# A hybrid encoder on one core: attention scores in two matmuls over stacked query halves

## The chip, the cores and the metric

One core of a Trainium2 chip runs the whole program once. The metric is the device time of one execution in microseconds (us). TensorE multiplies matrices into PSUM (eight banks of 128 partitions by 512 words), VectorE and ScalarE read PSUM and SBUF, GpSimd (POOL) works on SBUF and also issues DMAs, and SyncE (SP) issues the loads of the weights.

## The reference, cut to what matters

Four layers, each a token mixer and a gated feed-forward with a short convolution, both behind an RMS norm and with a residual. Mixers: convolution, neighbourhood attention, retention, convolution. The change lies in the attention of the second layer (512 tokens on a grid of 8 rows by 64 columns, 16 heads of 64):

```python
q = rmsnorm(qkv[:, :, 0], q_g) * (NAT_HEAD_DIM ** -0.5)
k = rmsnorm(qkv[:, :, 1], k_g)
...
sc = jnp.einsum('bhqd,bhrqwd->bhqrw', q_r, k_win).astype(jnp.float32)
sc = sc + bias.transpose(0, 2, 1, 3)[None].astype(jnp.float32)
p = jax.nn.softmax(sc.reshape(b, NAT_HEADS, GRID_W, kh * NAT_KW), axis=-1)
...
return jnp.einsum('bhqrw,bhrqwd->bhqd', p, v_win)
```

A token sees all 8 rows and a window of 16 columns.

## The kernel before, in words

Every product of float32 values is made of float32r parts: a value is split into a high part (rounded by ScalarE) and a low part (the rest, by VectorE), and a product is high by high, high by low and low by high, three matmuls into one PSUM bank (`mm3`, lines 151 to 154; `mm3s`, lines 156 to 159, with the operands' roles exchanged; `split`, lines 161 to 163).

The activations stand transposed in SBUF, channels in the partitions. Weights come by SP's queue into two raw buffers (L138) and are split (L147, L148).

The attention stage (`nat`) takes the heads in four groups of four. The list `NORDER` gives the order in which the steps are written down: `p0 a0 p1 a1 p2 w0 a2 p3 a3 w1 w2 w3`, where `p` is a group's projection, `a` its attention and `w` its share of the output projection. Within that, a planner orders each engine's instructions: it runs through the program with a timing model and takes what is ready, in the order written down, so that matmuls of a later projection come between those of an attention. What each engine then runs is fixed before the start, and each engine takes its instructions in order.

- `proj` (L505): queries, keys and values of a group, 96 matmuls of 256 columns each (L157 to L159). Queries and keys are evacuated by ScalarE (L512) into `qk`, squared on POOL (L517), summed on VectorE (L518) and scaled on POOL (L531). The values are split, and two DMAs on POOL's queue make a copy `vs` shifted by 64 partitions (L544, L545).
- `att_prep` (L548): for each of the two head pairs of a group, TensorE transposes queries and keys (L555) into PSUM, two heads of 64 channels in 128 partitions. Keys become `kh` and `kl` (L558, L559). Queries become `qz`: for each head a tile with its own 64 rows filled and the other 64 rows zero, so that a product over all 128 rows takes one head alone. The zero rows are filled once, at the stage's start (L485 to L488), for two sets of tiles.
- `att_pair` and `att_step` (L569, L589): for each head and each half of the queries, two blocks of 128 queries by 256 keys: three matmuls each (L596), the bias with mask and the row's extreme in one VectorE instruction (L603), the exponential (L606), the scaling (L614), four transposes (L616), the split into `ph`, `pl`, and the product with the values.
- PSUM has three banks for projections and five for attention. All preparation of a group is written before its two pairs (`PRE`).
- `wout` (L637): a group's share of the output, with residual adds on VectorE (L234); the last one is followed by the norm for the feed-forward.

Of the kernel before, what the change touches and what calls it, by code (L numbers as in the profile page):

```python
# [8 lines left out]
F32 = mybir.dt.float32  # L9
F32R = mybir.dt.float32r  # L10
I32 = mybir.dt.int32
AF = mybir.ActivationFunctionType
ALU = mybir.AluOpType
AX = mybir.AxisListType
MUL, ADD, SUB = ALU.mult, ALU.add, ALU.subtract
PSUM = bass.MemoryType.PSUM

P = 128
T = 512
# [39 lines left out]
NORDER = "p0 a0 p1 a1 p2 w0 a2 p3 a3 w1 w2 w3".split()  # L59
NRAW = 2  # L60
HPO = 100000
NQZ = 2


@with_exitstack
def tile_trunk(
# [7 lines left out]
    nc = tc.nc  # L74
# [9 lines left out]
    def nm(s):  # L84
        uid[0] += 1
        return f"{s}{uid[0]}"
# [36 lines left out]
    def pc(name, i=0, w=1):  # L123
        c = COLS[name] + i
        if c < 64:
            return png[:, c:c + w]
        return pt[:, c:c + w]
# [23 lines left out]
    def mm3(o, wh, wl, ah, al, first, last):  # L151
        nc.tensor.matmul(o, wh, ah, start=first, stop=False)  # L152
        nc.tensor.matmul(o, wh, al, start=False, stop=False)  # L153
        nc.tensor.matmul(o, wl, ah, start=False, stop=last)  # L154
# [317 lines left out]
    def nat(after):  # L472
        PER = 4
        with ExitStack() as st:
            stage_pools(st, NTMP, *NPS)
            np1 = st.enter_context(tc.tile_pool(name=nm("nat"), bufs=1, reuse_waits=RW))
# [1 line left out]
            mask = np1.tile([P, 3, 256], F32, tag="mask", name=nm("mask"))  # L478
            nc.scalar.dma_start(mask, nmask.rearrange("p (v k) -> p v k", v=3))
            kstart = (0, 64, 192, 256)  # L480
            qzs = [[np1.tile([P, 2, T], F32R, tag=f"qz{n}{i}", name=nm("qz")) for i in range(2)]
                   for n in range(NQZ)]
            zz = np1.tile([P, 1], F32, tag="zz", name=nm("zz"))
            nc.vector.memset(zz, 0.0)
            for qz in qzs:  # L485
                for i in range(2):
                    zp = slice(64 - 64 * i, 128 - 64 * i)
                    nc.vector.tensor_copy(qz[i][zp], zz[zp].unsqueeze(2).broadcast_to([64, 2, T]))  # L488

            def part_proj(g, part):  # L490
                pss = [bank(psa), bank(psa)]
# [54 lines left out]
                return qk, va, vs  # L546

            def att_prep(g, pi, qk):  # L548
                qz = qzs[(2 * g + pi) % NQZ]
                kh = np2.tile([P, T], F32R, tag="kh", name=nm("kh"))  # L550
                kl = np2.tile([P, T], F32R, tag="kl", name=nm("kl"))
                for part in range(2):
                    ps = bank(psb)
                    for tb in range(4):
                        nc.tensor.transpose(ps[:, tb * P:(tb + 1) * P],  # L555
                                            qk[:, part, tb, pi * P:(pi + 1) * P], ident)
                    if part == 1:
                        nc.scalar.activation(kh, ps, AF.Copy, scale=pc("kg"))  # L558
                        nc.vector.scalar_tensor_tensor(kl, ps, pc("kg"), kh.bitcast(F32), MUL, SUB)  # L559
                    else:  # L560
                        for i in range(2):
                            r = slice(64 * i, 64 * i + 64)
                            nc.scalar.activation(qz[i][r, 0, :], ps[r], AF.Copy, scale=pc("qg")[r])
                            nc.vector.scalar_tensor_tensor(
                                qz[i][r, 1, :], ps[r], pc("qg")[r], qz[i][r, 0, :].bitcast(F32),
                                MUL, SUB)
                return qz, kh, kl

            def att_pair(g, pi, qz, kh, kl, va, vs):  # L569
                hi = np1.tile([P, T], F32R, tag="oh", name=nm("oh"), bufs=NO)  # L570
                lo = np1.tile([P, T], F32R, tag="ol", name=nm("ol"), bufs=NO)
                bms = []
                for i2 in range(2):
                    W = np2.tile([P, 384], F32, tag="W", name=nm("W"))
                    nc.sync.dma_start(W, wd[g * PER + pi * 2 + i2])
                    bm = np1.tile([P, 3, 256], F32, tag="bm", name=nm("bm"), bufs=NBM)
                    for vi, ws in enumerate((128, 64, 0)):
                        nc.gpsimd.tensor_tensor(bm[:, vi, :], W[:, ws:ws + 256],
                                                mask[:, vi, :], ADD)
                    bms.append(bm)  # L580
                for pr in range(2):
                    for i2 in range(2):
                        r = slice(64 * i2, 64 * i2 + 64)
                        c = slice(pr * 256, pr * 256 + 256)
                        op = att_step(pi, i2, pr, qz, kh, kl, bms[i2], va, vs)
                        split(op, hi[r, c], lo[r, c])
                return hi, lo

            def att_step(pi, i2, pr, qz, kh, kl, bm, va, vs):  # L589
                hh = pi * 2 + i2  # L590
                S = bank(psb)
                for i in range(2):
                    b = pr * 2 + i
                    ks = slice(kstart[b], kstart[b] + 256)
                    qs = slice(b * P, (b + 1) * P)
                    mm3(S[:, i * 256:(i + 1) * 256], qz[i2][:, 0, qs], qz[i2][:, 1, qs],  # L596
                        kh[:, ks], kl[:, ks], True, True)
                e = np1.tile([P, T], F32, tag="e", name=nm("e"), bufs=NE)
                mn, sx, rx = sm(2), sm(2), sm(2)
                for i in range(2):  # L600
# [490 lines left out]
```

## Time and profile before

| | us |
|---|---|
| median of three runs | 2616.24 (2616.24 to 2617.13) |
| profiled execution | 2615.78 |
| its span | 2614.0 |
| TensorE busy | 2583.8 |
| VectorE busy | 1643.6 |
| ScalarE busy | 1047.9 |
| POOL busy | 239.7 |

The span runs from the first to the last instruction of the profiled execution. Matmul times in the profile are pipelined and overlap: a matmul listed with 0.28 us can be followed by the next after less than half of that, and the distance between two starts tells what one costs. In a row of the timeline stand start, duration, engine, line, operation, the tiles out<-in, the shape, and in brackets the engine's idle time before it with what ended that. The attention stage runs from about 598 to 848 us of the span.

### The profile page before, as it was taken

The numbers are of one execution on the slowest core, as the hardware profiler recorded it, in microseconds if no ns is written. First come the engines' busy times: TensorE is split into PE (matmuls) and PEld (weight loads), VectorE is DVE, ScalarE is ACT, GpSimd is POOL, SyncE is SP. The second block draws the span as 40 slices with busy tenths as digits, with TensorE's granted clock in tenths as the row PEclk, the third lists the DMA queues.
The fourth block names the chain that finished last, engine by engine and source line by source line (L and its number), as shares of the span: only waits on it lengthen the run. The fifth ranks groups of instructions, "written<-read, shape, count | busy, mean of one in ns | idle before, by whom it ended". The sixth has DMA issues, their size and how long they took to land.

```text
span 2614.0 us, 32452 instructions
## 1 busy us (share of the span) xinstructions
PE 2583.8 (99%) x12830; PEld 2150.4 (82%) x12830; DVE 1643.6 (63%) x2628; ACT 1047.9 (40%) x1425; POOL 239.7 (9%) x253
## 2 busy tenths in 40 slices
PE   9989999999999999999999999999999998999999
PEld 7978888889998788888888888888888887888888
DVE  6766777437878777634656566677733667677732
ACT  5444444335655444423332423444432444444421
POOL 0104000003422000000000000100000100100000
PEclk9999999999999999999999999999999999999999
DMA  7624222333232222233222221322233652222232
GB/s 250 207 100 143 97 93 93 96 91 117 87 91 81 93 95 91 93 97 108 81 81 73 81 81 58 103 89 97 95 89 108 226 195 72 89 97 92 92 109 79
DMA packets 79784, 275.10 MB, mean 105 GB/s; under 512 B 10080, under 2 KB 13024, under 8 KB 79632
## 3 DMA queue, kind: packets, MB, share of 16 engines
q1 hardware_dynamic: 74304, 259.18, 30.4%
q0 software_dynamic: 4032, 11.14, 1.5%
q10 hardware_dynamic: 1296, 2.72, 0.3%
q8 instruction: 100, 1.64, 0.3%
q14 instruction: 52, 0.43, 0.0%
HBM read 263.04 MB, written 5.63 MB: 103 GB/s over the span
## 4 chain that ended last, share of the span: by engine, by line
PE 98%; DVE 1%; issue 0%; DMA 0%; ACT 0%; POOL 0%; SPq 0%; DVEq 0%; POOLq 0%
PE ps L154 27%; PE ps L152 27%; PE ps L153 27%; PE ps L393 3%; PE ps L158 3%; PE ps L159 3%; PE ps L157 3%; PE ps L396 1%; PE ps L289 1%; PE ps L290 1%; PE ps L294 1%; PE ps L616 0%; PE ps L437 0%; PE ps L842 0%; PE ps L555 0%
## 5 line engine op out<-in xcount | busy, mean ns | idle before, releaser
L147 ACT CAST wh<-wr 128x1024 fp32r<-128x1024 f32 (+1 forms) x410 | 423.2, 1034 | 1097.4 <-PE ps L153 801.0
L154 PE MATMUL ps<-xh,wl 128*128 128x512 f32 x1856 | 739.4, 398 | 0.0
L152 PE MATMUL ps<-xh,wh 128*128 128x512 f32 x1856 | 731.1, 394 | 6.3 <-ACT xh L201 6.3
L153 PE MATMUL ps<-xl,wh 128*128 128x512 f32 x1856 | 732.8, 395 | 0.0
L148 DVE TENSOR_TENSOR wl<-wr,wh 128x1024 fp32r<-128x1024 f32 (+1 forms) x406 | 493.3, 1215 | 329.1 <-ACT wh L147 326.8
L152 PEld LDWEIGHTS ps<-xh,wh 128*128 128x128 f32 x1856 | 349.1, 188 | 89.1 <-ACT xh L201 6.3
L153 PEld LDWEIGHTS ps<-xl,wh 128*128 128x128 f32 x1856 | 349.1, 188 | 87.7
L154 PEld LDWEIGHTS ps<-xh,wl 128*128 128x128 f32 x1856 | 349.0, 188 | 81.1
L152 PE MATMUL ps<-hh,wh 128*128 128x512 f32 (+1 forms) x726 | 281.6, 388 | 0.5 <-DVE x L316 0.5
L153 PE MATMUL ps<-hl,wh 128*128 128x512 f32 (+1 forms) x726 | 281.5, 388 | 0.0
L154 PE MATMUL ps<-hh,wl 128*128 128x512 f32 (+1 forms) x726 | 281.4, 388 | 0.0
L261 DVE TENSOR_TENSOR t<-ps,rstd_bc 128x512 f32<-128x512 f32 x176 | 120.9, 691 | 163.5 <-PE ps L154 163.5
L217 POOL TENSOR_TENSOR sqacc<-t,sqacc 128x512 f32<-128x512 f32 x49 | 77.5, 1581 | 1285.7 <-ACT t L215 1285.0
L152 PEld LDWEIGHTS ps<-hh,wh 128*128 128x128 f32 x726 | 136.8, 188 | 30.7 <-DVE x L316 0.7
L153 PEld LDWEIGHTS ps<-hl,wh 128*128 128x128 f32 x726 | 136.8, 188 | 30.1
L154 PEld LDWEIGHTS ps<-hh,wl 128*128 128x128 f32 x726 | 136.8, 188 | 30.0
L158 PE MATMUL ps<-wl,xh 128*128 128x256 f32 (+1 forms) x512 | 159.2, 312 | 0.6 <-DVE wl L148 0.6
L159 PE MATMUL ps<-wh,xl 128*128 128x256 f32 (+1 forms) x512 | 159.2, 312 | 0.0
L157 PE MATMUL ps<-wh,xh 128*128 128x256 f32 (+1 forms) x512 | 158.5, 312 | 0.0
L264 ACT ACTIVATE t<-t,par 128x512 f32<-128x512 f32 x176 | 142.5, 814 | 5.8 <-DVE t L261 5.7
L268 DVE SCALAR_TENSOR_TENSOR t<-t,par,t 128x511 f32<-128x511 f32 x176 | 132.1, 751 | 5.8
L393 PE MATMUL ps<-W,X 128*128 128x256 f32 x576 | 134.2, 331 | 0.6 <-DVE W L163 0.6
(227 smaller groups left out, 3470.1 us busy)
## 6 DMA issues: line engine op xcount, KB each, us to landing
wr<-in_f_up SPq DMA_DIRECT2D x176, 512.0 KB, 3.3
wraw<-in_cdw SPq DMA_DIRECT2D x64, 576.0 KB, 4.8
wr<-in_f_down SPq DMA_DIRECT2D x64, 448.0 KB, 3.3
wr<-in_f_down SPq DMA_DIRECT2D x32, 512.0 KB, 3.5
wr<-in_cw_in SPq DMA_DIRECT2D x30, 512.0 KB, 3.6
wr<-in_nat_qkv SPq DMA_DIRECT2D x24, 512.0 KB, 3.3
wr<-in_cw_out SPq DMA_DIRECT2D x16, 512.0 KB, 3.6
wr<-in_ret_qk SPq DMA_DIRECT2D x16, 512.0 KB, 3.2
```

What stands on the lines that cost most here:

```text
L147: nc.scalar.copy(hi[:, :n], raw[:, :n])
L148: eng.tensor_tensor(lo[:, :n], raw[:, :n], hi[:, :n].bitcast(F32), SUB)
L152: nc.tensor.matmul(o, wh, ah, start=first, stop=False)
L153: nc.tensor.matmul(o, wh, al, start=False, stop=False)
L154: nc.tensor.matmul(o, wl, ah, start=False, stop=last)
L157: nc.tensor.matmul(o, ah, wh, start=first, stop=False)
L158: nc.tensor.matmul(o, ah, wl, start=False, stop=False)
L159: nc.tensor.matmul(o, al, wh, start=False, stop=last)
L261: nc.vector.tensor_tensor(u, ps, rstd_bc, MUL)
L264: nc.scalar.activation(a, u, AF.Identity, bias=pc("fdb", l * 44 + c), scale=pt[:, w + 1:w + 2])
L268: nc.vector.scalar_tensor_tensor(a[:, :T - 1], u[:, 1:], pt[:, w + 2:w + 3], a[:, :T - 1], MUL, ADD)
L393: nc.tensor.matmul(o, X[:, b, 0, a:a + P], W[:, a].rearrange("p h n -> p (h n)"), start=a == 0, stop=False)
```

## The change

The scores of a head are made of two matmuls. The queries of a head stand in one tile `qs` of 128 rows: the high part in 64 rows and the low part in the other 64. The keys of a head stand twice, above one another: `ks` holds in both halves of the partitions the same 64 channels, high part and low part beside one another. Queries (high over low) times key high parts, plus queries times key low parts, gives the three products and the low by low product as well.

Keys are evacuated into a staging tile `kt` (one buffer), and four DMAs on POOL's queue copy it into the two `ks` tiles of the pair. VectorE writes the query low parts into the other half of the partitions. Keys are prepared before queries. The zero fills go away.

```diff
-            qzs = [[np1.tile([P, 2, T], F32R, tag=f"qz{n}{i}", name=nm("qz")) for i in range(2)]
-                   for n in range(NQZ)]
-            zz = np1.tile([P, 1], F32, tag="zz", name=nm("zz"))
-            nc.vector.memset(zz, 0.0)
-            for qz in qzs:
-                for i in range(2):
-                    zp = slice(64 - 64 * i, 128 - 64 * i)
-                    nc.vector.tensor_copy(qz[i][zp], zz[zp].unsqueeze(2).broadcast_to([64, 2, T]))
...
             def att_prep(g, pi, qk):
-                qz = qzs[(2 * g + pi) % NQZ]
-                kh = np2.tile([P, T], F32R, tag="kh", name=nm("kh"))
-                kl = np2.tile([P, T], F32R, tag="kl", name=nm("kl"))
-                for part in range(2):
+                qs = [np2.tile([P, T], F32R, tag=f"q{i}", name=nm("q")) for i in range(2)]
+                ks = [np2.tile([P, 2, T], F32R, tag=f"k{i}", name=nm("k")) for i in range(2)]
+                kt = np1.tile([P, 2, T], F32R, tag="kt", name=nm("kt"))
+                halves = (slice(0, 64), slice(64, 128))
+                for part in (1, 0):
...
                     if part == 1:
-                        nc.scalar.activation(kh, ps, AF.Copy, scale=pc("kg"))
-                        nc.vector.scalar_tensor_tensor(kl, ps, pc("kg"), kh.bitcast(F32), MUL, SUB)
+                        nc.scalar.activation(kt[:, 0], ps, AF.Copy, scale=pc("kg"))
+                        nc.vector.scalar_tensor_tensor(
+                            kt[:, 1], ps, pc("kg"), kt[:, 0].bitcast(F32), MUL, SUB)
+                        for i in range(2):
+                            for r in halves:
+                                nc.gpsimd.dma_start(ks[i][r], kt[halves[i]])
                     else:
-                        for i in range(2):
-                            r = slice(64 * i, 64 * i + 64)
-                            nc.scalar.activation(qz[i][r, 0, :], ps[r], AF.Copy, scale=pc("qg")[r])
+                        for i, r in enumerate(halves):
+                            nc.scalar.activation(qs[i][r], ps[r], AF.Copy, scale=pc("qg")[r])
                             nc.vector.scalar_tensor_tensor(
-                                qz[i][r, 1, :], ps[r], pc("qg")[r], qz[i][r, 0, :].bitcast(F32),
+                                qs[i][halves[1 - i]], ps[r], pc("qg")[r], qs[i][r].bitcast(F32),
                                 MUL, SUB)
...
-                    mm3(S[:, i * 256:(i + 1) * 256], qz[i2][:, 0, qs], qz[i2][:, 1, qs],
-                        kh[:, ks], kl[:, ks], True, True)
+                    o = S[:, i * 256:(i + 1) * 256]
+                    nc.tensor.matmul(o, q[:, qs], k[:, 0, ks], start=True, stop=False)
+                    nc.tensor.matmul(o, q[:, qs], k[:, 1, ks], start=False, stop=True)
```

## Rows read from the trace of the kernel before

**Rows 1.** The page: busy time of the engines (share of the span, instructions), and the chain that ended last by engine.

```profile
PE 2583.8 (99%) x12830; PEld 2150.4 (82%) x12830; DVE 1643.6 (63%) x2628; ACT 1047.9 (40%) x1425; POOL 239.7 (9%) x253
...
PE 98%; DVE 1%; issue 0%; DMA 0%; ACT 0%; POOL 0%; SPq 0%; DVEq 0%; POOLq 0%
```

**Rows 2.** The table by stretch of the attention stage. Columns: stretch, its length, busy time (and instructions) of PE, PEld, DVE, ACT and POOL, granted clock of TensorE, DMA share, GB/s.

```profile
608.00:680.00 72.00, 71.51 (x653) 71.51 (x654) 56.34 (x150) 39.72 (x89) 28.36 (x30) 1.00 0.31 96
680.00:735.00 55.00, 55.00 (x505) 54.40 (x505) 44.58 (x119) 33.82 (x79) 19.62 (x22) 1.00 0.31 94
735.00:797.00 62.00, 62.00 (x535) 60.06 (x534) 49.02 (x127) 35.33 (x79) 18.42 (x22) 1.00 0.30 90
797.00:831.00 34.00, 34.00 (x228) 29.34 (x227) 32.60 (x88) 18.92 (x47) 6.46 (x9) 1.00 0.33 98
831.00:850.00 19.00, 14.73 (x90) 11.17 (x88) 14.89 (x23) 12.28 (x24) 8.94 (x5) 1.00 0.14 50
```

**Rows 3.** What TensorE waited for from 597 to 850 us: who, for whom, us in total, times, longest.

```profile
PE ps L152 <- DVE pl L163: 1.2, 2, 1.1
PE ps L158 <- DVE wl L148: 0.6, 1, 0.6
PE ps L616 <- DVE e L614: 0.6, 1, 0.6
PE ps L152 <- ACT oh L162: 0.5, 1, 0.5
```

**Rows 4.** The timeline of TensorE in the first group: two score matmuls in succession.

```profile
638.22 0.28 PE L153 MATMUL ps<-kl,qz 128*128 128x256 f32 x1
638.34 0.28 PE L154 MATMUL ps<-kh,qz 128*128 128x256 f32 x1
```

**Rows 5.** The timeline of TensorE in a projection: the first and the last of 27 matmuls of the same shape that follow one another.

```profile
683.00 0.28 PE L158 MATMUL ps<-wl,xh 128*128 128x256 f32 x1
...
686.05 0.28 PE L159 MATMUL ps<-wh,xl 128*128 128x256 f32 x1
```

**Rows 6.** The table by stretch of the matmuls that read the padded queries `qz`: busy time and number on PE, granted clock, DMA share, GB/s.

```profile
608.00:680.00 72.00, 6.59 (x48) 1.00 0.31 96
680.00:735.00 55.00, 6.90 (x48) 1.00 0.31 94
735.00:797.00 62.00, 7.20 (x48) 1.00 0.30 90
797.00:831.00 34.00, 7.01 (x48) 1.00 0.33 98
```

**Rows 7.** The timeline of VectorE at the start of the attention stage.

```profile
598.20 5.10 DVE L488 CAST qz<-zz 64x1024 fp32r<-64x1024 f32 x4
...
607.21 1.23 DVE L148 TENSOR_TENSOR wl<-wr,wh 128x1024 fp32r<-128x1024 f32 x1
```

**Rows 8.** Timelines around the groups: on PE the last matmul of the first group's attention, the second group's transposes, the place from which its scores follow one another, the first of its later scores, the last matmul of the third group's attention and the fourth group's first transposes; on DVE and POOL the second group's preparation.

```profile
674.80 0.22 PE L154 MATMUL ps<-ph,va 128*64 128x128 f32 x1
...
680.78 1.91 PE L555 MATMUL ps<-ident,qk 128*128 128x128 f32 x16
...
683.99 0.74 DVE L564 SCALAR_TENSOR_TENSOR qz<-ps,par,qz 64x512 fp32r<-64x512 f32 x1
684.65 0.73 DVE L559 SCALAR_TENSOR_TENSOR kl<-ps,par,kh 128x512 fp32r<-128x512 f32 x1
...
686.28 0.55 POOL L544 DMA_DIRECT2D vs<-va  x1 [8.89 <-DVE va L163]
...
689.82 0.28 PE L152 MATMUL ps<-kh,qz 128*128 128x256 f32 x1
...
706.03 0.28 PE L152 MATMUL ps<-kh,qz 128*128 128x256 f32 x1
...
776.84 0.22 PE L154 MATMUL ps<-ph,va 128*64 128x128 f32 x1
...
785.62 0.60 PE L555 MATMUL ps<-ident,qk 128*128 128x128 f32 x4
```

**Rows 9.** The two copies of the values on POOL's queue, by line: number, duration of the issue in ns (min/median/max), and the time from issue to landing.

```profile
L544 POOL DMA_DIRECT2D vs<-va x4: 551/551/592, 635.4 to 799.9; - x4
...
DMA to landing us min/median/max: 3.6/3.7/6.6
...
L545 POOL DMA_DIRECT2D vs<-va x4: 534/538/542, 636.0 to 800.5; - x4
...
DMA to landing us min/median/max: 4.9/5.3/7.8
```

**Rows 10.** The timeline of VectorE in the last group, between the transposes and the first softmax step.

```profile
797.70 0.74 DVE L564 SCALAR_TENSOR_TENSOR qz<-ps,par,qz 64x512 fp32r<-64x512 f32 x1
...
803.59 0.41 DVE L603 CUSTOM_DVE_ANT_0 e<-ps,bm 128x256 f32<-128x256 f32 x1
```

**Rows 11.** Timelines of VectorE and POOL in the first group's softmax: two pairs of scalings, and what POOL ran beside the second.

```profile
641.01 0.61 DVE L614 TENSOR_SCALAR e<-e,sm 128x256 f32<-128x256 f32 x2
...
642.68 1.39 DVE L614 TENSOR_SCALAR e<-e,sm 128x256 f32<-128x256 f32 x2
642.84 1.09 POOL L517 TENSOR_TENSOR t<-qk 128x512 f32<-128x512 f32 x1 [6.33 <-ACT qk L512]
```

**Rows 12.** All waits for a DMA on POOL's copies in the convolution stages: us in total, times, longest.

```profile
ACT X L162 <- DMA xf<-u: 11.2, 10, 2.8
```

More of the change, by code (lines that the diff above doesn't have):

```diff
@@ L61 @@
 HPO = 100000
-NQZ = 2
 @with_exitstack
@@ L557, in att_prep, with att_pair @@
                     if part == 1:
-                        nc.scalar.activation(kh, ps, AF.Copy, scale=pc("kg"))
-                        nc.vector.scalar_tensor_tensor(kl, ps, pc("kg"), kh.bitcast(F32), MUL, SUB)
-                    else:
-                        for i in range(2):
-                            r = slice(64 * i, 64 * i + 64)
-                            nc.scalar.activation(qz[i][r, 0, :], ps[r], AF.Copy, scale=pc("qg")[r])
+                        nc.scalar.activation(kt[:, 0], ps, AF.Copy, scale=pc("kg"))
[4 more added lines that the diff above has]
+                                nc.gpsimd.dma_start(ks[i][r], kt[halves[i]])
+                    else:
+                        for i, r in enumerate(halves):
+                            nc.scalar.activation(qs[i][r], ps[r], AF.Copy, scale=pc("qg")[r])
                             nc.vector.scalar_tensor_tensor(
-                                qz[i][r, 1, :], ps[r], pc("qg")[r], qz[i][r, 0, :].bitcast(F32),
+                                qs[i][halves[1 - i]], ps[r], pc("qg")[r], qs[i][r].bitcast(F32),
                                 MUL, SUB)
-                return qz, kh, kl
-            def att_pair(g, pi, qz, kh, kl, va, vs):
+                return qs, ks
+            def att_pair(g, pi, qs, ks, va, vs):
                 hi = np1.tile([P, T], F32R, tag="oh", name=nm("oh"), bufs=NO)
@@ L584, in att_pair, with att_step @@
                         c = slice(pr * 256, pr * 256 + 256)
-                        op = att_step(pi, i2, pr, qz, kh, kl, bms[i2], va, vs)
+                        op = att_step(pi, i2, pr, qs[i2], ks[i2], bms[i2], va, vs)
                         split(op, hi[r, c], lo[r, c])
                 return hi, lo
-            def att_step(pi, i2, pr, qz, kh, kl, bm, va, vs):
+            def att_step(pi, i2, pr, q, k, bm, va, vs):
                 hh = pi * 2 + i2
```

## The prediction

> **What bounds the kernel now.** I read the page's totals first, then the chain, then a table by stretch of the attention stage, then TensorE's waits in it. TensorE is busy 2583.8 of 2614.0 us and is 98% of the chain that ended last [rows 1]: an instruction taken from it pays wherever no other wait stands behind it, and one added elsewhere costs nothing until TensorE waits for it. The average is not enough, because the change lies in one stage of some 250 us. The table by stretch [rows 2] parts that stage. From 608 to 797 us TensorE is busy almost without a break, with VectorE at 78 to 81%: this part is TensorE's. From 797 to 831 both are full: VectorE is busy 32.60 of 34.00 us, so there a shorter TensorE stream leaves VectorE's work as it is. From 831 to 850 TensorE is idle for 4 us behind the last softmax. TensorE's listed waits from 597 to 850 sum to 2.9 us [rows 3], none of them for a DMA.
>
> **The change part by part.**
>
> *Removed: one matmul of three in every score.* 16 heads by 4 query blocks by 3 make 192 score matmuls; 128 stay. The 0.28 us beside each is a pipelined time; what one costs is the distance between starts. Two score matmuls start 0.12 us apart [rows 4]; the same shape in the projection has 26 distances between 683.00 and 686.05 us [rows 5], so 3.05 / 26 = 0.1173 us each. The new matmuls have this shape too (128 rows by 128 columns, 256 moving), so 64 x 0.1173 = 7.5 us leave TensorE. Each of four stretches holds 48 of the 192 [rows 6]: three are TensorE's (48 removed, 5.6 us); the last is the full one (16 removed, 1.9 us), of which I count nothing.
>
> *Removed: four fills of the zero padding.* They hold VectorE from 598.20 to 603.3; the root of the mean square and the low half at 607.21 stand behind them [rows 7]. TensorE works on meanwhile and waits only 0.6 us for that low half [rows 3]. So 5.1 us of VectorE are worth 0.6 us.
>
> *Moved: keys before queries.* In the second group's evacuations VectorE makes a query low half at 683.99 and the first key low half at 684.65 [rows 8]. With keys first, the key takes the 683.99 place and ends at 684.7, 0.7 us earlier, which pays for part of what follows. The number of these instructions stays: two for keys, four for queries in each pair.
>
> *Added: 32 copies on the POOL queue*, four for each of eight pairs, 64 partitions by 4096 bytes, 256 KB each. The nearest rows are the two 384 KB copies of the values on this queue: 0.55 and 0.54 us to issue; the first lands 3.7 us after its issue (3.6 to 6.6), the second 5.3 (4.9 to 7.8) [rows 9]. The second is issued 0.55 later, so it adds 5.3 + 0.55 - 3.7 = 2.15 us for 384 KB, or 1.4 us for 256 KB. From that I estimate the first key copy down after 3.7 - 0.7 = 3.0 us, the second 4.4, the third 5.9, the fourth 7.3. Head 0 of a pair needs the first two, head 1 all four. In the second group: 684.7 + 4.4 = 689.1 for head 0, where before the bulk of the scores began at 689.82 [rows 8]. In the last group the first low half after the transposes sits at 797.70 on VectorE and ends at 798.4; + 4.4 = 802.8, and before the first softmax step on VectorE was at 803.59 [rows 10]. In between VectorE has other low halves, a value split and residual adds to do, and the row at 803.59 names no idle time before it, so it does not run dry. Both ends for all 32: nothing, if other matmuls cover the wait; and, if every group's first score stood still for 7.8 - 3.7 = 4.1 us (from the median landing of the first row to the longest of the second), 16.4 us in four groups. I take nothing, the value nearest to rows 3, where no DMA holds TensorE.
>
> *Added: a wait on ScalarE.* The staging tile has one buffer, so the second pair of a group writes its key only when the first pair's four copies are down, 7.3 us later. Behind that instruction stand weight halves and exponentials on ScalarE, and one bank of the five stays taken. But the second pair's scores come late anyway: in the second group the last three of eight steps started only at 706.03 [rows 8]. The ends are nothing (the order is planned with the wait in view) and 7.3 us in each of four groups, 29 in all. I take nothing, because a group's attention ends well before the next group's transposes: 674.80 to 680.78 us and 776.84 to 785.62 [rows 8], 6 and 9 us to spare.
>
> *POOL itself* was busy 239.7 us of the span [rows 1]; 32 x 0.55 = 17.6 us of issuing come to it. Before the second group's value copies it had been idle for 8.89 us, waiting for a low half of the values [rows 8]; key copies put behind those in POOL's queue would wait too. Its ends are nothing and 17.6 us; I take nothing for the idle time.
>
> *A rule weighed.* Beside a POOL product of 1.09 us two of VectorE's scalings of the exponentials take 1.39 us instead of 0.61 [rows 11]: the two engines shut each other out. The Trainium skill (SBUF — State Buffer, "SBUF: two separate sides") goes further: while VectorE runs an operation in a two-port mode, GpSimd cannot write the descriptors of a DMA issued from its queue; the same page, under "A bandwidth-pool intuition that's wrong", has 620 ns alone against some 3100 ns. By that, the first copies of four groups would come 10 us late in all, an estimate from that page, and the sum below would end at 2620. In this trace VectorE runs evacuations and splits, not scalings, where a group's first copies fall [rows 10].
>
> **Sum.** -5.6 (three groups) - 0.6 (fills) + 0 = -6.2 us. The profiled execution took 2615.78 us, 1.78 more than its span of 2614.0, so 2609.6; the median of the runs, 2616.24, stands 0.46 above it: **2610.0 us**.
>
> **The rivals.**
> 1. *The copies are partly late.* For it: in the convolution stage ScalarE waited ten times for a like copy from POOL, 11.2 us in all, 1.1 each, 2.8 the longest [rows 12], so the planned order reckons such copies somewhat early; and the value copies may stand ahead in POOL's queue. Against it: none of those waits is among TensorE's in rows 3. At 1.1 us in each of four groups the gain is 6.2 - 4.4 = 1.8: 2614.4 us, which can't be told from no change.
> 2. *Slower: the copy of the keys becomes the bound.* The place is a group's first score on TensorE, which takes its instructions in order, so all behind it stands still. The price is the 4.1 us above in each of four groups: 2616.24 - 6.2 + 16.4 = 2626.4. Above 1.55 us a group it eats the gain; from 2.85 us a group it is slower by 0.2%. For it: landings of 6.6 and 7.8 us are in rows 9, and ScalarE's wait for the staging tile can hold weight halves back. Against it: the 6 and 9 us to spare in rows 8.
> 3. *Slower in another way: POOL and VectorE shut each other out* while the second head's and the second pair's copies are issued. Each of four issues would stand behind one pair of scalings, 4 x 1.39 = 5.6 us [rows 11]; in the two groups with the fewest other matmuls that is 11.1 us: 2616.24 - 6.2 + 11.1 = 2621.1. It is what that rule of the Trainium skill (SBUF — State Buffer) comes to here. Against it: the value copies in rows 9 were mostly down in 3.7 and 5.3 us.
> 4. *The last stretch gains too*, if VectorE's backlog there gets shorter because the work in front of it starts earlier: 2610.0 - 1.9 = 2608.1.
>
> That the change does not do what it says is hardly possible: a matmul that is not issued takes no time. The order of all engines is planned anew, though, and for that I allow 3 us either way.
>
> **How the numbers follow.** A difference of 0.2%, 5.2 us, is about what a measurement of this kernel can tell from none: faster is below 2611.0, slower above 2621.5. Chances: the forecast 0.36, with a range of its own from 2607 to 2613; rival 1 0.36; rival 2 0.15; rival 3 0.03; rival 4 0.10. Faster is rival 4 and all but a small edge (0.02) of the forecast, 0.44; same is rival 1 and that edge, 0.38; slower is rivals 2 and 3, 0.18. The range goes below to rival 4 less the 3 us for a changed order, 2605, and above into rival 2 as far as 3.0 us in each of four groups, 2622.
>
> **What would show it.** The score lines should hold 128 matmuls 0.117 us apart, the fills be gone, and TensorE's waits between 597 and 850 name no key copy. The time from the last group's transposes to the stage's end should be as before; the 6 us should lie ahead of them. TensorE waiting for a key tile or its DMA by over 1 us a group speaks for rival 1 or 2; ScalarE waiting on the staging tile with weight halves late behind it would show my zero for that wait wrong; VectorE idle ahead of the last group's first softmax would show the backlog argument wrong.

## The result, and the profile after

The changed kernel takes 2622.28 us (median of 20 runs, 2617.73 to 2625.64) against 2616.37 for the kernel before: ratio 1.0021, 95% interval 1.0014 to 1.0027, 5.9 us slower. The forecast was 2610.0 with a range up to 2622, and slower had a chance of 0.18: the sign was wrong, and the time lies just outside the range. The spread of the 20 runs goes with TensorE's mean granted clock in each, from 2617.7 us at 0.997 to a median of 2624.8 in the four runs at 0.994.

The page of the changed kernel, busy times and the chain by engine, against [rows 1]:

```profile
PE 2583.5 (99%) x12766; PEld 2145.1 (82%) x12766; DVE 1641.5 (63%) x2623; ACT 1045.3 (40%) x1425; POOL 257.2 (10%) x285
...
PE 93%; DVE 4%; DMA 1%; ACT 1%; issue 1%; POOL 0%; SPq 0%; ACTq 0%; POOLq 0%; DVEq 0%
```

64 matmuls are gone (12830 to 12766), and TensorE's busy time is what it was. The idle rest of the span grew from 30.2 to 37.3 us, and the busy time is a union of pipelined matmuls, which hides that some stand further apart. The chain tells it: TensorE's share fell from 98% to 93%, and VectorE, DMA and ScalarE came in.

The table by stretch, columns as in [rows 2]:

```profile
608.00:680.00 72.00, 69.75 (x619) 67.51 (x618) 54.44 (x148) 37.80 (x87) 32.55 (x37) 1.00 0.44 125
680.00:735.00 55.00, 53.88 (x493) 52.82 (x492) 43.66 (x117) 32.13 (x77) 27.41 (x32) 1.00 0.46 125
735.00:797.00 62.00, 58.50 (x484) 55.50 (x483) 49.34 (x125) 31.62 (x74) 22.17 (x30) 0.97 0.48 128
797.00:831.00 34.00, 32.74 (x193) 27.62 (x193) 29.68 (x63) 17.86 (x39) 9.63 (x17) 1.00 0.66 163
```

The stretches are the same times, not the same work. In each of these TensorE now has gaps (3.5 us in the third, none before), and the DMA engines carry more than before: 0.44 to 0.66 against 0.30 to 0.33. What the gaps wait for, TensorE's waits from 590 to 870 us, against [rows 3]:

```profile
PE ps L592 <- DMA k<-kt: 4.9, 4, 3.2
PE ps L612 <- DVE e L610: 3.3, 8, 1.1
PE ps L288 <- DVE x L233: 2.2, 1, 2.2
PE ps L151 <- DVE pl L162: 1.8, 5, 0.7
```

The first line is new: scores (L592) wait for the DMA that copies the keys. The second had 0.6 us, once; now the transposes of the scaled exponentials wait eight times. (The third, behind the last residual add, stands with the same 2.2 us in all kernels below, third_off among them, and is no part of the change.) The copies by their line, with the time from issue to landing:

```profile
L555 POOL DMA_DIRECT2D k<-kt x32: 509/529/604, 633.1 to 816.4; - x32
...
  ACT kt L550: 11.4, 3
  PE ps L592: 4.9, 4
...
DMA to landing us min/median/max: 2.9/5.1/10.0
```

The 4.9 us are not the whole. Read from both timelines, the time from the start of a group's main block of transposes to its first score matmul, in the four groups (in the first and the fourth, the kernel before had run four of the sixteen transposes 9 us ahead of that block):

```
before   5.9   5.4   4.5   5.3 us
after   10.1  10.2  12.1  10.4 us
```

By that measure each group's scores start 4 to 8 us later. TensorE has other work for most of that, but the softmax that follows on VectorE starts later too. The first projection matmul and the last output matmul of the stage, in the kernel before and in the changed one:

```profile
594.44 0.28 PE L157 MATMUL ps<-wh,xh 128*128 128x256 f32 x1
847.60 0.39 PE L154 MATMUL ps<-oh,wl 128*128 128x512 f32 x1
...
594.34 0.28 PE L156 MATMUL ps<-wh,xh 128*128 128x256 f32 x1
854.57 0.40 PE L153 MATMUL ps<-oh,wl 128*128 128x512 f32 x1
```

The stage grew from 253.2 to 260.2 us, although the 7.5 us of removed matmuls are gone: some 14.6 us of distance between TensorE's starts came in.

The third group is the worst. POOL's timeline there, and TensorE's:

```profile
738.48 0.55 POOL L535 DMA_DIRECT2D vs<-va  x1 [5.42 <-DVE va L162]
739.03 0.54 POOL L536 DMA_DIRECT2D vs<-va  x1
739.74 2.02 POOL L555 DMA_DIRECT2D k<-kt  x4 [0.17 <-issue]
```

```profile
745.46 0.40 PE L153 MATMUL ps<-oh,wl 128*128 128x512 f32 x1
749.05 0.42 PE L592 MATMUL ps<-k,q 128*128 128x256 f32 x1 [3.20 <-DMA k<-kt]
749.28 0.42 PE L593 MATMUL ps<-k,q 128*128 128x256 f32 x1
...
749.92 0.63 PE L151 MATMUL ps<-oh,wh 128*128 128x512 f32 x1
750.35 0.63 PE L152 MATMUL ps<-ol,wh 128*128 128x512 f32 x1
```

Two value copies left just ahead of the key copies; the keys of the first head landed at 748.96, 9.2 us after 739.74. In the other groups it was 5.3, 5.1 and 6.1 us, where the prediction had 4.4. The table over the wait and what follows it, columns as before:

```profile
740.00:745.60 5.60, 5.60 (x28) 4.45 (x26) 5.22 (x8) 3.10 (x4) 1.76 (x4) 1.00 1.09 243
745.60:749.00 3.40, 0.25 (x2) 0.00 (x0) 1.84 (x3) 0.00 (x0) 0.00 (x0) 1.00 1.08 237
749.00:752.50 3.50, 3.45 (x11) 2.90 (x12) 0.78 (x4) 0.21 (x1) 0.00 (x0) 0.53 0.32 89
752.50:756.00 3.50, 3.50 (x30) 3.50 (x29) 3.08 (x7) 2.52 (x6) 0.13 (x1) 0.98 0.18 28
```

While the copies were under way, with a weight load on SP's queue beside them, the DMA engines were full (1.09 and 1.08). And after its 3.2 us of idleness TensorE ran at a granted clock of 0.53, the 1.2 GHz level, for 3.5 us: the products with 512 columns start 0.43 us apart instead of 0.235. From 749.05 to 752.48 it did four scores and six of these, which at the full clock take 4 x 0.117 + 6 x 0.235 = 1.88 us: 1.55 us more for the one wait.

### The profile page after: what moved, and what is told of

Read it like the earlier page. It is cut to its first block, busy times and chain, and to the rows that moved or that the text cites. A ratio compares the mean times of both kernels' runs of the same rounds, so it can differ in the third digit from the quotient of the medians.

```text
span 2620.8 us, 32404 instructions
## 1 busy us (share of the span) xinstructions
PE 2583.5 (99%) x12766; PEld 2145.1 (82%) x12766; DVE 1641.5 (63%) x2623; ACT 1045.3 (40%) x1425; POOL 257.2 (10%) x285
## 3 DMA queue, kind: packets, MB, share of 16 engines
q1 hardware_dynamic: 74304, 259.18, 30.2%
## 4 chain that ended last, share of the span: by engine, by line
PE 93%; DVE 4%; DMA 1%; ACT 1%; issue 1%; POOL 0%; SPq 0%; ACTq 0%; POOLq 0%; DVEq 0%
PE ps L153 26%; PE ps L151 26%; PE ps L152 26%; PE ps L392 4%; PE ps L158 2%; PE ps L156 2%; PE ps L157 2%; PE ps L395 1%; DMA k<-kt 1%; DVE e L610 1%; DVE wl L147 1%; PE ps L288 1%; PE ps L289 1%; PE ps L293 1%; PE ps L436 0%
```

## The experiments

The theory behind the experiments was that the time from a ready key to its landing is what is paid. Rivals: issuing on POOL, the wait for the staging tile, the order keys before queries, and the stacked layout itself.

**no_copies**: the changed kernel without copies; both heads read the evacuated keys.

```diff
-                ks = [np2.tile([P, 2, T], F32R, tag=f"k{i}", name=nm("k")) for i in range(2)]
-                kt = np1.tile([P, 2, T], F32R, tag="kt", name=nm("kt"))
+                kt = np2.tile([P, 2, T], F32R, tag="kt", name=nm("kt"))
+                ks = [kt, kt]
...
-                        for i in range(2):
-                            for r in halves:
-                                nc.gpsimd.dma_start(ks[i][r], kt[halves[i]])
```

> The changed kernel without its 32 key copies and without the single staging buffer: both heads read the evacuated keys where they lie (two buffers). It leaves out that each head's keys stand in both halves, so its scores mix two heads; the 128 score matmuls, the stacked queries and the order keys before queries stay. Theory A (the copies: their landing, the staging buffer and the order planned around them cost some 14 us of the stage, more than the 7.5 us that the matmuls give): 2608 to 2611 us, and TensorE's idle time in the stage back near the kernel before. Theory B (the copies are not the cause: softmax on VectorE and the order of work bound the stage, so that fewer matmuls only turn into waits for the exponentials): 2616 us or more.

2614.24 us; ratio 0.9991 (0.9983 to 1.0). The copies cost 8.0 us. But the gain that remains, 2.5 us, is far from the forecast: something else is paid too. The first scores stand 7.0, 7.0, 5.9 and 5.9 us behind the transposes here, so 1 to 2 us of their delay in the changed kernel come without any copy.

**third_off**: the kernel before with two of its three matmuls; the product of the queries' low part is left out.

```diff
-                    mm3(S[:, i * 256:(i + 1) * 256], qz[i2][:, 0, qs], qz[i2][:, 1, qs],
-                        kh[:, ks], kl[:, ks], True, True)
+                    o = S[:, i * 256:(i + 1) * 256]
+                    nc.tensor.matmul(o, qz[i2][:, 0, qs], kh[:, ks], start=True, stop=False)
+                    nc.tensor.matmul(o, qz[i2][:, 0, qs], kl[:, ks], start=False, stop=True)
```

> The kernel before with zero padding and everything else as it was, but only two of the three matmuls of each score: the low part of the queries is left out (and still computed). It measures the removal by itself. Theory A: 64 x 0.117 = 7.5 us less, or 5.6 if the last group's part is not gained: 2609 to 2611 us. Theory B: within 2 us of 2616.

2608.71 us; 0.997 (0.9959 to 0.9982): 8.0 us less. By the profile the stage takes 245.9 us instead of 253.2, 7.3 less: all 64 matmuls count, those of the last stretch too.

**copies_3mm**: the kernel before, its padding and 192 matmuls kept, with keys first, a staging tile and four copies of 128 KB a pair.

```diff
-                for part in range(2):
+                for part in (1, 0):
...
+                            for r in halves:
+                                nc.gpsimd.dma_start(ks[r, i], kt[r, i])
```

> The kernel before with all its zero padding and 192 score matmuls, but keys evacuated first, into a staging tile of one buffer, and copied by four DMAs of a pair on the POOL queue into the tile that the scores read (64 partitions by 2048 bytes each, half the bytes of the changed kernel's). It measures the copies without the removal. Theory A: 2616 plus most of 14 us, 2625 to 2631; at half the bytes the landings are shorter, so 2622 is the lower end. Theory B: within 2 us of 2616.

2619.67 us; 1.001 (1.0001 to 1.0019): +2.9. Here no score waits for a DMA; its copies are half as large, those of the high parts leave before the low parts are made, and they land in 2.2 to 5.8 us, median 3.6. So not every copy costs 8 us, which comes back in the last pair of runs. The time fits neither theory, and the first scores come 8.2 to 9.3 us behind the transposes, nearly as late as in the changed kernel: a late first score alone doesn't set the price.

**inplace**: no staging tile; each head's keys are evacuated into their own half, one copy of 256 KB a head fills the other.

```diff
+                        for i, r in enumerate(halves):
+                            nc.scalar.activation(ks[i][r, 0], ps[r], AF.Copy, scale=pc("kg")[r])
+                            nc.vector.scalar_tensor_tensor(
+                                ks[i][r, 1], ps[r], pc("kg")[r], ks[i][r, 0].bitcast(F32), MUL, SUB)
+                            nc.gpsimd.dma_start(ks[i][halves[1 - i]], ks[i][r])
```

> The changed kernel without the staging tile: each head's keys are evacuated into their own half of the head's tile (one more ScalarE and one more VectorE instruction a pair, 0.69 and 0.74 us, 5.5 and 5.9 us in all), and one copy a head brings them to the other half: 16 copies instead of 32, half the bytes, and no wait of ScalarE for a staging buffer. Theory A, if the staging wait and the number of copies matter: 2611 to 2617 us, with ScalarE's wait for the copies gone. If the landing of the first copy alone matters: 2618 to 2622, since a group's first scores still stand behind a copy. Theory B: 2622 to 2626, for VectorE has more to do.

2622.7 us; 1.0022 (1.0012 to 1.0031), the same as the changed kernel with half the copies, and without ScalarE's 11.4 us of waiting for the staging tile. So no gain from ending that wait shows; since a pair has one more instruction here on ScalarE and one on VectorE, a small gain may be hidden. TensorE's wait for keys is still there, and larger:

```profile
PE ps L590 <- DMA k<-k: 7.8, 5, 2.9
```

**third_kfirst**: third_off with keys first (`for part in (1, 0)`).

> The kernel before without each score's third matmul (the queries' low part is left out of the scores, as in the run third_off, 2608.7 us) and with one line more: keys are evacuated before queries. Theory O (the order keys before queries costs some 5 us by itself, since all transposes of a group then wait for the keys, which are projected after the queries): 2613 to 2615 us, and the fourth group's sixteen transposes in one block after its value projection. Rival L (the order is free; what run no_copies lost against third_off comes from the stacked layout or its buffers): 2608 to 2610 us.

2613.14 us; 0.9987 (0.9978 to 0.9996). Against third_off the order costs 4.4 us, with no copy in the kernel; TensorE's waits for the split of the exponentials are 2.2 us instead of 0.5. **no_copies_qf** asks the same of the stacked layout: no_copies with queries first.

> Run no_copies (2614.2 us) with queries before keys; what it leaves out is the same, the key copies. If the order of keys and queries is worth the 4.4 us that third_kfirst and third_off lie apart, also in the stacked layout: 2608.5 to 2611 us. If the stacked layout or the missing fills hold something of their own: 2612 to 2615.

2608.28 us; 0.9969 (0.9958 to 0.998): 6.0 us under no_copies, and next to third_off. The stacked layout itself costs nothing.

**q_first**: the changed kernel with queries first.

> The changed kernel with one line different: queries are evacuated before keys, as in the kernel before. Theory O: 5 us less than the changed kernel, 2616 to 2619 us, less what the later start of the key copies gives back. Rival L, with the landing of the copies as the only price: the keys start 0.7 to 1.5 us later on ScalarE and VectorE in each of four groups, so 2622 to 2627 us.

2620.64 us; 1.0015 (1.0006 to 1.0024). Only 1.6 us come back, between the ranges of the two theories: the keys, and with them the copies, start later.

**early_keys**: key preparation and copies written ahead of the group's value projection.

```diff
+                kks = [key_prep(pi, qk) for pi in range(2)]
                 pvs = part_proj(g, 2)
```

> The changed kernel with the key half of the preparation (transposes, evacuation, copies) written ahead of the group's value projection instead of behind it, so that 11 us of projection matmuls stand between the copies and the scores; queries are prepared where they were. Theory C (the copies' landing in front of a group's scores costs some 8 us, the distance of the changed kernel from run no_copies): 2612 to 2616 us, with TensorE's waits for a key copy gone. Rival (not the landing but POOL's and ScalarE's queues behind the copies): 2619 to 2623 us, with no wait for a copy on TensorE all the same.

2618.8 us; 1.0007 (0.9998 to 1.0016), 3.5 us under the changed kernel. TensorE's waits for keys fell to 2.8 us only, and the time misses the theory's 2612 to 2616. **early_all** moves the whole preparation (queries first) to that place, and **before_early** does so in the kernel before.

```diff
+                pre = [att_prep(g, pi, qk) for pi in range(2)]
                 pvs = part_proj(g, 2)
```

> The changed kernel with a group's whole preparation, queries first, then keys and copies, written ahead of the group's value projection; nothing is left out. If the landing in front of the scores is the loss of the changed kernel (theory L) and the rest of early_keys' loss was the queries' work behind the projection: like no_copies_qf, 2607 to 2611 us, with no wait of TensorE for a copy in the first three groups. If the copies cost beside the landing (staging buffer, PSUM banks held): 2615 to 2620 us, as early_keys (2618.8).

> The kernel before with the same move and nothing else: the preparation of queries and keys ahead of the group's value projection. If the move itself is worth something, because VectorE's low halves leave the last group's full stretch: 2612 to 2615 us; if it only serves to hide a landing, which this kernel does not have: within 1.5 us of 2616.6.

2622.88 us (1.0025, 1.0015 to 1.0036) and 2619.07 (1.0009, 1.0 to 1.0018). Both lie outside both of their ranges, and the move doesn't help: 2.2 us more than q_first, which has the same order, and 2.5 more than the kernel before. The keys aren't there earlier. POOL's timeline of early_all in the last group:

```profile
795.23 2.04 POOL L522 TENSOR_TENSOR qk<-qk,sm 128x512 f32<-128x512 f32 x2 [5.89 <-DVE sm L174]
```

The scaling of the keys ends at 797.3 behind VectorE's root of the sums, when the value projection has 1.6 us to go, and twelve of the sixteen transposes stand behind that projection, from 799.25. Where a step is written matters little if its input is late. What early_keys gained stays unexplained.

**copies_unread**: all 32 copies are issued, into two tiles that nothing reads; the scores read the evacuated keys, of which there are two buffers, as in no_copies.

```diff
+                kd = [np1.tile([P, 2, T], F32R, tag=f"kd{i}", name=nm("kd")) for i in range(2)]
+                kt = np2.tile([P, 2, T], F32R, tag="kt", name=nm("kt"))
+                ks = [kt, kt]
...
+                                nc.gpsimd.dma_start(kd[i][r], kt[halves[i]])
```

> The changed kernel with its 32 copies issued as before, of the same size and on the same queue, but into two tiles that nobody reads; the scores read the staging tile, which has two buffers here, as in run no_copies (the heads' keys are mixed in the scores). Theory L (TensorE and the softmax behind it stand because a group's scores wait for the copies to land): like no_copies, 2613 to 2616 us. Theory Q (the copies cost by being issued: POOL's queue, its shared port with VectorE, the DMA engines): like the changed kernel, 2620 to 2623 us.

2610.39 us; 0.9977 (0.9968 to 0.9985). This parts issuing from waiting: the same copies, landing in 3.8 to 8.9 us, cost nothing if no score waits for them, and 11.9 us (to 2622.28) if one does. It is also 3.9 us faster than no_copies, which does less. In the profiles the stage accounts for 1.0 us of that (249.0 against 250.0), which may be the new plan; the rest arises behind the stage and is taken up under the sum.

**copies_sp**: the copies on SP's queue.

```diff
-                                nc.gpsimd.dma_start(ks[i][r], kt[halves[i]])
+                                nc.sync.dma_start(ks[i][r].bitcast(F32), kt[halves[i]].bitcast(F32))
```

> The changed kernel with the key copies on SP's queue instead of POOL's, between the weight loads. The value copies can then not stand ahead of them, POOL is free for its own products, and the bias tables on the same queue landed in 2.4 us in the kernel before. Theory L, with the landing as the price: the landing falls from 4.4 us and more to 3, and the third group's wait of 3.4 us with its slow clock goes: 2615 to 2619 us. If weights behind a waiting copy come late, waits of ScalarE for raw weights appear: 2620 us or more.

2634.22 us; 1.0072 (1.0058 to 1.0086). Landing 2.9/4.7/9.7 us is no shorter, an issue took up to 2.3 us, ScalarE's wait for the staging tile grew from 11.4 to 27.2 us, and TensorE's waits grew:

```profile
PE ps L592 <- DMA k<-kt: 13.3, 5, 4.0
```

**direct_high**: no copies, queries first. ScalarE writes the key's high part into both halves, and its low part takes a product over 64 rows.

```diff
+                    nc.tensor.matmul(o, q[:, qs], k[:, ks], start=True, stop=False)
+                    h = slice(64 * i2, 64 * i2 + 64)
+                    nc.tensor.matmul(o, q[h, qs], kl[h, ks], start=False, stop=True)
```

> Two score matmuls without any copy, queries first: only the keys' high part stands in both halves, written there twice by ScalarE from PSUM (three more instructions a pair, 3 x 0.69 x 8 = 16.6 us of ScalarE less the one it replaces by halves), the keys' low part stays in one half and its product runs over the query high part's 64 rows alone. All three products are there. Theory O + C (order and copies are the whole loss): 2608 to 2612 us, like third_off, with the zero fills gone too. If ScalarE's and VectorE's added instructions (one more on VectorE, 0.74 x 8 = 5.9 us, against 5.1 us of fills) bound the last group: 2612 to 2617 us. If a product over 64 rows is slower than one over 128: 64 x the difference of starts above 0.117 us.

2642.56 us; 1.0101 (1.0087 to 1.0116). A surprise, which TensorE's timeline explains:

```profile
639.05 0.28 PE L593 MATMUL ps<-k,q 128*128 128x256 f32 x1
639.26 0.38 PE L595 MATMUL ps<-kl,q 64*128 64x256 f32 x1
639.57 0.38 PE L593 MATMUL ps<-k,q 128*128 128x256 f32 x1
639.88 0.38 PE L595 MATMUL ps<-kl,q 64*128 64x256 f32 x1
```

Matmuls over 64 and 128 rows in turn start 0.31 us apart instead of 0.117. 128 times 0.19 is 25 us. The distances are not all: in two places TensorE's granted clock fell to 0.50, the 1.2 GHz level, for 6.8 us, each time behind 6.4 us in which 18 or 19 of the 28 matmuls were such ones. The first of the two, columns as in the table by stretch, here and at the same time in direct_pad, the next kernel:

```profile
645.40:652.20 6.80, 6.80 (x29) 6.15 (x29) 2.44 (x12) 3.55 (x11) 2.02 (x3) 0.50 0.08 32
645.40:652.20 6.80, 6.80 (x60) 6.80 (x59) 5.39 (x20) 4.57 (x14) 4.14 (x4) 1.00 0.21 77
```

**direct_pad** keeps the scheme, with the key's low part in a tile of 128 rows of which 64 are zero.

```diff
-                    nc.tensor.matmul(o, q[h, qs], kl[h, ks], start=False, stop=True)
+                    nc.tensor.matmul(o, q[:, qs], kl[:, ks], start=False, stop=True)
```

> Run direct_high (2642.6 us) with its second product over 128 rows again: the keys' low part stands in 64 rows of a tile whose other 64 rows are zero, filled once (half as many zeros as in the kernel before). In direct_high a matmul over 64 rows beside one over 128 started 0.31 us after its neighbour instead of 0.117; 128 distances by 0.19 us are 25 us. If those are all of its loss: 2617 us less what the rest gains, 2612 to 2618 us. If the added ScalarE and VectorE instructions cost nothing: 2609 to 2612. It does the whole computation without a copy.

2615.56 us; 0.9997 (0.9988 to 1.0005): 27 us come back with the shape, its clock included; how they divide between distances and clock stays open. It does the three products with two matmuls and no copy, in the time of the kernel before.

**parts** and **parts_qf**: inplace with each head's copy cut in two of 128 KB; the high part leaves as soon as ScalarE has written it. Keys first, then queries first.

```diff
                         for i, r in enumerate(halves):
                             nc.scalar.activation(ks[i][r, 0], ps[r], AF.Copy, scale=pc("kg")[r])
+                            nc.gpsimd.dma_start(ks[i][halves[1 - i], 0], ks[i][r, 0])
+                        for i, r in enumerate(halves):
                             nc.vector.scalar_tensor_tensor(
                                 ks[i][r, 1], ps[r], pc("kg")[r], ks[i][r, 0].bitcast(F32), MUL, SUB)
-                            nc.gpsimd.dma_start(ks[i][halves[1 - i]], ks[i][r])
+                            nc.gpsimd.dma_start(ks[i][halves[1 - i], 1], ks[i][r, 1])
```

> inplace with each head's copy cut in two of 128 KB: the high part leaves as soon as ScalarE has it, the low part follows. All products as in the changed kernel. Theory (the time from a ready key to its landing is what the change pays): landings near the 3.6 us that the 128 KB copies took in copies_3mm, instead of 6.1 in inplace, TensorE's waits for a key copy fall from 7.8 to under 4 us, and the time from 2622.7 to 2614 to 2619 us. Rival (the price is the plan made around any copy, whatever its landing): 2620 to 2625 us.

> The same with queries first. If landing and order were both paid and small copies hide, 2610 to 2615 us, below the kernel before. If the copies, which now start later, are late for the first scores, as in q_first (2620.6): 2617 to 2622 us.

parts: 2613.7 us, just under the theory's 2614 to 2619 and far from the rival's; 0.999 (0.9981 to 0.9999). It computes all that the changed kernel computes and is 8.6 us faster, and 3.0 faster than the kernel before (2616.73 beside it), the fastest here that leaves nothing out. The stage of its profile is less than 1 us shorter than before, 252.3 against 253.2; the rest lies outside it. TensorE's wait for keys fell from 7.8 us to this:

```profile
PE ps L593 <- DMA k<-k: 0.8, 1, 0.8
```

The landings did not fall to 3.6 us as expected (medians 4.2 for the high parts, 5.3 for the low), but the high parts leave earlier. POOL's timeline of parts in the third group:

```profile
734.00 0.55 POOL L551 DMA_DIRECT2D k<-k  x1 [6.24 <-ACT k L550]
734.54 0.54 POOL L535 DMA_DIRECT2D vs<-va  x1
735.07 0.52 POOL L536 DMA_DIRECT2D vs<-va  x1
735.57 0.53 POOL L551 DMA_DIRECT2D k<-k  x1
```

The first key copy now goes ahead of the value copies, and the first score, which needs the high part alone, runs 7.3 to 7.7 us after the transposes in the first, second and fourth group, instead of 10. parts_qf: 2622.16 us; 1.0019 (1.001 to 1.0028); TensorE's waits for keys sum to 4.2 us. Its first key copy of the third group left behind the value copies again, and the landing medians were 5.9 and 6.6 us. So the small copies gain nothing with queries first (q_first has 2620.64), and the edits can't be priced apart: keys first gains 8.5 us with these small copies, costs 1.6 with the large ones (q_first) and 4.4 to 6.0 without any.

## Why the prediction was wrong

**The removed matmuls: right in kind, too small.** 0.1173 us each, 64 of them, is 7.5; third_off gained 8.0. The step that was wrong is "the last is the full one (16 removed, 1.9 us), of which I count nothing". In third_off the time from the last group's transposes to the last product with the values fell from 43.4 to 41.0 us. Before and in third_off, columns as in [rows 2]:

```profile
794.60:838.00 43.40, 41.60 (x293) 35.51 (x291) 38.47 (x97) 24.39 (x59) 8.76 (x9) 1.00 0.31 92
789.15:830.15 41.00, 39.85 (x277) 33.96 (x275) 38.61 (x97) 24.19 (x59) 8.92 (x9) 1.00 0.32 97
```

VectorE runs 97 instructions in either, 38.5 and 38.6 us, so its idle time fell, from 4.9 to 2.4 us: nearly full from 797 to 831 us [rows 2], it was not the limit of the group as a whole. Rival 4 had the size, but of a kernel without copies, and by luck: VectorE's work in the group did not get less.

**The zero fills.** TensorE's 0.6 us of waiting for that low half is gone. In the time nothing is to be seen of it: no_copies, with the fills gone, stands 1.1 us above third_kfirst, which has them.

**Keys before queries.** Predicted as a step that "pays for part of what follows". Alone, it costs 4.4 us (third_kfirst) or 6.0 (no_copies_qf against no_copies). In third_off four transposes for the last group run at 780.26, 9 us ahead of the other twelve; with keys first all sixteen stand in one block at 789.65. I moved the key's instruction into the query's place on VectorE and left the rest of the plan as it was. In the profiles the stage pays 4.0 us for it in the one layout and 4.3 in the other. How much of that belongs to the order and how much to this plan stays open.

**The copies.** "I take nothing, the value nearest to rows 3, where no DMA holds TensorE" is the step that failed: it turned the sign. Rows 3 could not show a wait that the kernel before doesn't have. The sum of the pieces was half right: the estimate of 4.4 us to the first head's landing was 0.7 to 1.7 us short in three groups and 4.8 in the third. The worse error was what I held it against. For the second group I compared the landing, 689.1, with 689.82, from where the scores follow one another; the first score stood at 686.17 by the timeline, and it feeds the first softmax. In the last group it stood at 799.89, against a landing put at 802.8:

```profile
686.17 0.28 PE L152 MATMUL ps<-kh,qz 128*128 128x256 f32 x1
...
799.89 0.40 PE L152 MATMUL ps<-kh,qz 128*128 128x256 f32 x2
```

By my own numbers the copy was 2.9 us late for both, which in four groups is 11.6 us, an estimate from these rows. The measured price, from no_copies or copies_unread to the changed kernel, is 8.0 to 11.9 us.

**Rival 2** named the place, a group's first score, and its price of 16.4 us was the nearest of all, if too high; the measured 8 to 12 are 2 to 3 us a group. Its mechanism is shown only in part: TensorE stood still for 4.9 us; that the rest came as a later softmax is argued from the waits behind it, not tried, and copies_3mm, whose first scores are nearly as late, paid less. Parts shows that it is when the copies land, and not that there are copies; of its two edits, smaller pieces and an earlier first one, neither was run alone. **Rival 1**, at 4.4 us in all, was too small.

**The waits counted at zero.** ScalarE does wait for the staging tile, 11.4 us, and no run speaks against that zero (inplace, with the reserve made there). POOL's issuing held too (copies_unread). **Rival 3** didn't happen: the scalings of the exponentials take 32.4 us in all against 31.5 before. By the rule of the Trainium skill (SBUF — State Buffer, "SBUF: two separate sides") a copy's descriptors would be written late while VectorE runs an operation in a two-port mode. The issues took 0.60 us at the longest, and the latest landing fell where the DMA engines were full; no run here parts a late descriptor from a slow transfer.

**The sum, by the runs**: 2616.4 - 8.0 (third_off) + 4.4 (keys first) + 1.1 (layout and fills) + 8.0 (copies) = 2621.9, against 2622.3. The steps are differences of medians along one chain of kernels, so they have to add up within the drift of the kernel before (medians of 2616.37 to 2616.81); another path gives the same total with other shares.

The profiles, one execution each, part the stage from what lies behind it. From its first projection matmul to its last output matmul the stage takes 253.2 us before, 260.2 changed, 245.9 in third_off, 249.9 in third_kfirst, 250.0 in no_copies, 245.8 in no_copies_qf, 249.0 in copies_unread and 252.3 in parts. By these the removal gains 7.3 us, the order costs 4.0 to 4.3, the layout 0.1 either way, the copies 10.2 to 11.2. Behind the stage all kernels run the same 7930 matmuls, yet the first 200 take 49.9 us in some and 48.3 in others. The difference is TensorE's granted clock, which fell to the 1.2 GHz level for 3.4 us there in the first kind and not in the second. The first 8 us behind the stage, before and in third_off:

```profile
848.00:856.00 8.00, 5.87 (x19) 4.66 (x20) 8.00 (x7) 3.98 (x7) 7.69 (x5) 0.79 0.19 68
840.00:848.00 8.00, 5.84 (x26) 4.65 (x26) 8.00 (x7) 4.11 (x7) 7.69 (x5) 1.00 0.20 66
```

Of the second kind are third_off, copies_unread, before_early, parts and parts_qf. So 1.6 us of a difference between two profiles can come from the clock behind the stage, and a small difference between medians, such as the 3.0 us by which parts beats the kernel before, is not shown to be the stage's.

Of the signs named beforehand, 128 score matmuls and no fills were there; TensorE's line on a key copy, which was not to be there, was. VectorE did not run dry ahead of the last group's first softmax; ahead of the other three it waited 2.7 to 3.1 us for the scores, a place I hadn't named. The time from the last group's main block of transposes to the last output matmul, which was to stay as it was, grew from 53.0 to 54.4 us.

## What to carry to other kernels

Price a copy put between a producer and the matmuls by the time from its last input to its landing, and hold that against the first consumer, not against the bulk of them. Where it can't be hidden, try to cut it so that the part that is ready first leaves first, and ahead of other copies on its queue; here that paid with keys first and not with queries first. A busy time that stayed the same after work had been removed meant here that gaps had come in: look at the distances between starts. And compare the stage that was changed, not only the whole: here the clock behind it was worth 1.6 us.

## What the hardware showed that I had not expected

Matmuls over 64 rows and 128 rows in turn start 0.31 us apart, where either neighbour over 128 rows would start after 0.117; in direct_high that, with two stretches of 6.8 us at a granted clock of 0.50, cost 27 us against direct_pad. Six copies in a row (four of keys, two of values), with a weight load beside them, filled the DMA engines (share 1.09, 243 GB/s), and the landing of 256 KB, 2.9 us at the shortest in this kernel, took up to 10.0. A single 3.2 us wait cost TensorE 1.55 us more, because what followed ran at the 1.2 GHz level.
